# Four chunks of u normalized beside the last plain pair, two more squares on VectorE, and one low half issued later, in a hybrid attention, convolution and SwiGLU block

## The chip, the cores and the metric

The kernel runs on one core of one Trainium2 chip. The metric is the device time of one execution in microseconds (us). The kernel before was run three times. Beside those runs one execution was recorded by the hardware profiler; all durations and waits below come from that one.

## What is computed

One residual layer over 512 tokens of 2048 features, in float32. Cut to what matters here:

```python
u = rms_norm(h, mix_pre_g)
q, k, v, ca, cb, ga, gb = split(u @ w_in)
y_attn = neighbourhood_attention(q, k, v, rpb) @ w_attn_o
z = ca * sigmoid(cb)
z = depthwise_conv(z, w_dw, width=31) + b_dw
y_conv = silu(layer_norm(z, ln_g, ln_b)) @ w_conv_o
merged = sigmoid(ga) * y_attn + sigmoid(gb) * y_conv
h = h + rms_norm(merged @ w_out, mix_post_g)
u = rms_norm(h, ffn_pre_g)
gate, up = split(u @ w_gate_up)
h = h + rms_norm((silu(gate) * up) @ w_down, ffn_post_g)
```

## The kernel before

**Arithmetic.** Features lie on the 128 partitions and the 512 tokens along the free axis, so an activation is 16 tiles of 128x512. Every product of float32 values is made from halves: an operand is split into a high half (a cast to fp32r, on ScalarE, ACT) and a low half (the operand less its high half, on VectorE, DVE). A product then takes three matmuls: high by low, high by high, low by high. Weights are treated alike. `wchunk` loads 128x1024 values on SP's DMA queue into one of five buffers of the tag "raw" (L150), casts the high half on ACT (L151) and makes the low half on VectorE (L156). A raw buffer is free again when its low half has been made. `split` (L165) does the same for an activation, and `gemm` runs the three matmuls over eight k-tiles of each weight tile (L197, L200, L201).

**Taps.** The depthwise convolution has 31 taps for each of 8 tiles; each tap but the middle one is one VectorE instruction (`tap`, L470). They are not done in one go: `wchunk` ends with `taps(rate)`, which puts `rate` taps from a list behind each weight tile, in every stage from the plain pairs to the output projections. `R_CONV`, `R_V` (two halves), `R_QK` and `R_Y` set the rate by stage.

**Stages around the change.** First come the plain pairs of the gated convolution (`cb` and `ca`): tiles 0 and 1 are interleaved with the loading of x, and i = 2, 3, 4 take 16 k-tiles each for `cb` and then for `ca`. They use u without the row norm and scale the result. From v on, u is used with the norm applied: `normalize(c)` loads chunk c of x again into a raw buffer (L425, SP), multiplies it on VectorE (`un`, L526, two tiles), stores both tiles to DRAM (ACT's queue), and splits them (L165). Chunks 0 to UN_EARLY - 1 are normalized ahead of the last plain pair's weights, each other one ahead of its weights in v's first half. v has two halves of eight chunks, each of 24 matmuls (L555 to L557).

**w_out.** The product with w_out takes pairs of output tiles by a seven-product scheme of quarters (`strassen`): products named 11, 21, T2, T1, T3, 22 and T4 accumulate into banks x, y and z, with sums of weight quarters on VectorE between them (`wsum`, L280; `s4`, L341). In the first pair ("apart") the product 21 has a bank of its own. A sum p5 (L339) reads bank y after T3 and before T4 adds to it. Each product's weights get their halves in `halved_weights` (L258). The operands of the first pair come from `mr[i]`, whose last addition is on L879, followed by `operand_steps` (differences on L863, halves through `merged`, L178 and L179).

**Sum of squares.** For the FFN's norm, each of 16 tiles of the new h is squared on ACT (L977). Squares 0, 1 and KT - 4 = 12 start three accumulators; squares 2 to 11 are added to the first two by GpSimd (POOL) with accumulating DMAs (L981), and 13 to 15 to the third on VectorE (`folded`, L389). At the end VectorE adds the third and the second accumulator to the first. `rstd` sums over partitions with one-column matmuls (`r_s`, L362), VectorE scales (`r_v`, L370), GpSimd takes the power (`r_r`, L372), and `by_column` spreads the result with eight matmuls (`r_b`, L379); between `r_s` and `r_b` stand nine matmuls of the next product.

**Order.** Each engine runs its instructions in the order in which the build's scheduler puts them; where the code pins an instruction (`keep_in_program_order`) or ties it behind another (`issued_behind`), that order is fixed. Buffers of a tag go to whoever comes next in that order, when one is free.

Of the kernel before, what the change touches and what calls it, by code (L numbers as in the profile page):

```python
# [28 lines left out]
ALU = mybir.AluOpType  # L29
# [5 lines left out]
KT = D // P  # L35
# [22 lines left out]
DN_3 = DN_2 + DN_P  # L58

LN_AT = 10  # L60
R_CONV, R_V, R_QK, R_Y = 4, (3, 4), 4, 4
PLAIN = 5
TAP_K, TAP_AT = 2, ((1, 3, 5), (0, 1, 3, 5))
BEFORE = 14
# [6 lines left out]
SINGLE, SUMMED = 4, 10  # L71
COPY_AT = 10
RE_EARLY = 11
UN_EARLY, YA_EARLY = 2, 8
C_PRE, C_POST, C_FPRE, C_FPOST, C_LNG, C_LNB, C_BDW, C_WDW = 0, 16, 32, 48, 64, 72, 80, 88
C_N = C_WDW + CT * CW

# [2 lines left out]
def hybrid_block(ctx: ExitStack, tc, xT, vecs, rpb, mask, w_c0, w_qk, w_v, w_gg, w_cg, w_ao, w_co, w_out, w_g0, w_gu, w_dn, w_dl, g_post, out):  # L80
    nc = tc.nc
# [24 lines left out]
    def issued_behind(ins, other):  # L106

        tc.add_manual_dep(
            ins.ins, other.ins.name, mybir.DependencyInfo(mybir.DependencyClass.NoSync, mybir.DependencyReason.DATA),
            reason="issue order",  # L110
        )
# [139 lines left out]
        load(raw, w[:, c * 1024 : (c + 1) * 1024])  # L251
        return raw

    def halved_weights(w, name, pin=False):

        hi = wp.tile([P, 1024], F32R, tag="whi", name=f"{name}h")
        lo = wp.tile([P, 1024], F32R, tag="wlo", name=f"{name}l")
        ins = nc.scalar.copy(hi, w), nc.vector.tensor_tensor(out=lo, in0=w, in1=hi.bitcast(F32), op=ALU.subtract)  # L258
        for i in ins if pin else ():
            tc.keep_in_program_order(i)  # L260
        return hi, lo

    def begun(w0, name):
# [1 line left out]
        a11 = quarter(w0, 0, name)  # L265
        return (a11, *halved_weights(a11, name))

    def strassen(w0, w1, op, name, n, s1=None, behind_last=None, first=None, quarters=None, apart=False, turn=True, midway=None, taps_at=()):

        x, y, z = ((bank, abank)[n % 2](f"{name}_{i}") for i in range(3))

        def wsum(a, b, op, i):
            t = stp.tile([P, 1024], F32, tag="S", name=f"{name}s{i}")
            nc.vector.tensor_tensor(out=t, in0=a, in1=b, op=op)  # L280
            return t

        def copied(ps, i):
            t = stp.tile([P, NT], F32, tag="quad", name=f"{name}v{i}", bufs=3)
            nc.scalar.copy(t, ps)  # L285
            return t

        count = iter(range(7))

        def product(ps, w, b, first=False, last=False, lo_first=False):  # L290
            number = next(count)
            hi, lo = w if isinstance(w, tuple) else halved_weights(w, name)
            ws = [slice(k * P, (k + 1) * P) for k in range(HT)]
            steps = [(hi, slice(0, NT)), (lo, A)]
            if lo_first:
                steps.reverse()
            for n, (wt, cols) in enumerate(steps):
                for k, t in enumerate(op[b]):
                    mmul = nc.tensor.matmul(  # L299
                        ps[:, cols], wt[:, ws[k]], t[:, cols], start=first and n + k == 0,  # L300
                        stop=last and n + k == HT, skip_group_check=True,
                    )
                    if (n, k) == (0, TAP_K) and number in taps_at:
                        taps(1, mmul)

        def done(ps, i):
            t = stp.tile([P, HN], F32, tag="half", name=f"{name}c{i}", bufs=2)
            nc.scalar.copy(t, ps[:, B])
            return ps[:, A], t

        if quarters:
            a11, a12, a21, a22 = quarters
        elif apart:
            a11, a12, a21, a22 = (first[0], *(quarter(*w, name) for w in ((w0, 1), (w1, 0), (w1, 1))))
        s1 = s1 or sums(w1, name)
        if not apart:
            a11, a21, a12, a22 = (quarter(*w, name) for w in ((w0, 0), (w1, 0), (w0, 1), (w1, 1)))
        product(x, first[1:] if first else a11, "11", first=True)
        if apart:
            v = (bank, abank)[n % 2](f"{name}_3")  # L320
            product(v, a12, "21", first=True, last=True)
        s2 = wsum(s1, a11, ALU.subtract, 2)
        p1 = copied(x, 1)
        product(y, s2, "T2", first=True)
        product(z, s1, "T1", first=True)
        nc.vector.tensor_tensor(out=y, in0=y, in1=p1, op=ALU.add)  # L326
        u2 = copied(y, 2)
        s3 = wsum(a11, a21, ALU.subtract, 3)
        product(y, s3, "T3", lo_first=turn)
        if midway:  # L330
            midway()
        p5 = copied(z, 3)
        nc.vector.tensor_tensor(out=z, in0=z, in1=u2, op=ALU.add)
        if apart:
            nc.vector.tensor_tensor(out=v, in0=v, in1=p1, op=ALU.add)  # L335
            x = v
        else:
            product(x, a12, "21", last=True)
        nc.vector.tensor_tensor(out=p5, in0=y, in1=p5, op=ALU.add)  # L339
        s4 = s2  # L340
        nc.vector.tensor_tensor(out=s4, in0=a12, in1=s2, op=ALU.subtract)  # L341
        c11 = done(x, 1)
        product(z, s4, "22", last=True, lo_first=turn)
        c12 = None if behind_last else done(z, 2)
        product(y, a22, "T4", last=True)
        if behind_last:
            behind_last()
            c12 = done(z, 2)
        return c11, c12, done(y, 3), (p5[:, A], p5[:, B])
# [191 lines left out]
    u, v = un, []  # L541
# [125 lines left out]
    raw, uf, quarters = [], [], []  # L667
# [38 lines left out]
    first = (quarters[0], *halved_weights(quarters[0], "k0", pin=True))  # L706
# [168 lines left out]
    for i in (c + n * HT for c in range(HT) for n in range(2)):  # L875
        if i == KT - 1:
            first = begun(w_out[0], "wo0")
        mr[i] = gated(*projected(i, 1, w_co, yc))
        nc.vector.tensor_tensor(out=mr[i], in0=mr[i], in1=yg[i], op=ALU.add)  # L879

        if i < KT - 2:
            for _ in range(1 if i < HT else 5):
                next(steps[i % HT])
# [7 lines left out]
    acc = None  # L891
    for i in range(0, KT - 2, 2):
        c11, c12, c21, c22 = strassen(
            w_out[i], w_out[i + 1], op, f"wo{i}", i // 2 + 1, first=None if i else first, apart=i == 0
        )
        for n, halves_of in enumerate((((A, c11), (B, c12)), ((B, c22), (A, c21)))):
            t = slot(f"fo{i + n}")
            for cols, c in halves_of:
                joined(t[:, cols], c)
            nc.scalar.dma_start(f_d[i + n], t)  # L900
            acc = sumsq(acc, t, f"f{i + n}")
# [61 lines left out]
    for c in (*range(SPLIT), *range(HT)):  # L963
# [7 lines left out]
        for i in (2 * c, 2 * c + 1):  # L971
            h2(i, cols)
            if cols != A:
                nc.scalar.dma_start(h_d[i], f[i])

                sq = slot(f"h{i}_sq")
                nc.scalar.activation(sq, f[i], AF.Square)  # L977
                if i in (0, 1, KT - 4):
                    acc.append(sq)
                elif i < KT - 4:  # L980
                    nc.gpsimd.dma_start(acc[i % 2], sq, accum_op=ALU.add)  # L981
                else:
                    folded([acc[2], sq])
# [533 lines left out]
```

## Time and profile before

| | |
|---|---|
| median of three runs | 2481.27 us (2480.18, 2482.13, 2481.27) |
| the profiled execution's own time | 2482.7 us |
| its span in the trace | 2480.9 us |
| instructions | 35643 |
| accumulating loads' landing in the sum of squares | 5.0 to 8.8 us, median 6.7 |
| taps on z, L470 | x180, mean 765 ns |
| v weights, issue to landing | median 4.8 us |
| GpSimd's busy time | 479.5 us, 19% |

The span runs from the first to the last recorded instruction; the execution's own time has what lies around it as well. PE is TensorE's matmuls, PEld its weight loads (they overlap matmuls), DVE is VectorE, ACT is ScalarE, POOL is GpSimd, SP is SyncE, which only issues DMAs. A row of the timeline gives start, duration, engine, line, operation, output <- inputs, and in square brackets the idle time before it and what ended that. Two instructions of an engine overlap a little, so the cost of one in a full stretch is the distance between starts. Tile names are shown without their numbers where rows of several tiles are put together.

### The profile page before, as it was taken

How to read it: one execution, taken by the hardware profiler on the slowest of the kernel's cores; microseconds unless marked ns; L12 is line 12 of the kernel's file. 1: busy time of each engine (PE TensorE's matmuls, PEld its weight loads, DVE VectorE, ACT ScalarE, POOL GpSimd, SP SyncE). 2: the span in 40 equal slices, each digit the busy share in tenths (PEclk: the TensorE clock that was granted, in tenths of full speed). 3: DMA queues.
4: the chain of work that ended last, by engine and by line, in shares of the span. 5: the costliest groups of instructions: out<-in, count | busy, mean ns of one | idle time of the engine just before them, and what ended most of it. 6: DMA issues, size and time to landing. Idle time of an engine off the chain costs nothing. (4 is left out here: it accounts for less than half of the span.)

```text
span 2480.9 us, 35643 instructions
## 1 busy us (share of the span) xinstructions
PE 2458.6 (99%) x13219; PEld 2125.1 (86%) x13219; DVE 2081.9 (84%) x2754; ACT 1262.4 (51%) x1951; POOL 479.5 (19%) x576
## 2 busy tenths in 40 slices
PE   9999999999999999999999999999999999999998
PEld 8878888888888888889888888888888888888887
DVE  5998644998889778888898888889998889989886
ACT  5232333655555244556455555555555566456454
POOL 0102312200000000012111111122221203542343
PEclk9999999999999999999999999999999999999999
DMA  6363223766667544669466665666666678888987
GB/s 216 123 199 104 101 97 121 255 187 198 195 191 226 190 141 136 203 211 303 147 178 175 182 180 169 177 205 198 204 214 195 213 226 243 242 220 261 213 225 219
DMA packets 163246, 476.53 MB, mean 192 GB/s; under 512 B 18560, under 2 KB 28256, under 8 KB 163072
## 3 DMA queue, kind: packets, MB, share of 16 engines
q1 hardware_dynamic: 107200, 334.41, 40.3%
q0 software_dynamic: 34128, 101.86, 19.3%
q10 hardware_dynamic: 21744, 37.98, 4.1%
q8 instruction: 104, 1.70, 0.3%
q14 instruction: 70, 0.57, 0.1%
HBM read 400.52 MB, written 72.22 MB: 191 GB/s over the span
## 5 line engine op out<-in xcount | busy, mean ns | idle before, releaser
L470 DVE SCALAR_TENSOR_TENSOR cv<-z,vec,cv 128x497 f32<-128x497 f32 (+9 forms) x180 | 137.4, 765 | 2.8
L1054 POOL TENSOR_TENSOR row<-row,asq 128x512 f32<-128x512 f32 x30 | 55.0, 1832 | 407.6 <-ACT asq L1053 407.6
L156 DVE TENSOR_TENSOR wlo_qk<-raw_qk,whi_qk 128x1024 fp32r<-128x1024 f32 x32 | 41.2, 1287 | 61.7 <-ACT whi_qk L151 61.7
L1215 POOL TENSOR_TENSOR ys<-ys,row 128x512 f32<-128x512 f32 x32 | 57.7, 1804 | 115.8 <-DVE ys L352 107.1
L151 ACT CAST whi_qk<-raw_qk 128x1024 fp32r<-128x1024 f32 x32 | 33.6, 1051 | 81.2 <-PE qk L200 48.6
L1078 POOL TENSOR_TENSOR an<-an,row 128x512 f32<-128x512 f32 x32 | 52.2, 1631 | 75.4 <-DMA an<-a_d 49.1
L151 ACT CAST whi_y<-raw_y 128x1024 fp32r<-128x1024 f32 x31 | 32.6, 1052 | 66.4 <-PE py L200 50.9
L197 PE MATMUL py<-ycl,whi_y 128*128 128x512 f32 x128 | 49.8, 389 | 0.0
L200 PE MATMUL py<-ych,whi_y 128*128 128x512 f32 x128 | 49.8, 389 | 0.0
L201 PE MATMUL py<-ych,wlo_y 128*128 128x512 f32 x128 | 49.8, 389 | 0.0
L569 POOL TENSOR_TENSOR bm<-braw,msk 128x64 f32<-128x64 f32 x96 | 44.2, 496 | 28.7 <-DMA braw<-in_rpb 28.7
L156 DVE TENSOR_TENSOR wlo_y<-raw_y,whi_y 128x1024 fp32r<-128x1024 f32 x31 | 37.8, 1221 | 10.6 <-ACT whi_y L151 10.3
L470 DVE SCALAR_TENSOR_TENSOR cv<-zr,vec,cv 128x497 f32<-128x497 f32 (+14 forms) x60 | 45.3, 756 | 0.5
L480 POOL TENSOR_TENSOR csum<-csum,cv 128x512 f32<-128x512 f32 x7 | 12.1, 1734 | 144.4 <-DVE cv L470 144.4
L820 DVE TENSOR_TENSOR gg<-py,gg 128x512 f32<-128x512 f32 x32 | 21.7, 684 | 17.3 <-PE py L201 10.6
L631 POOL DMA_DIRECT2D att_d<-ao x8 | 4.4, 555 | 151.3 <-ACT ao L630 131.2
L606 ACT ACTIVATE sc<-sc,st 128x256 f32<-128x256 f32 x32 | 16.1, 504 | 31.4 <-DVE st L605 31.1
L1216 POOL DMA_DIRECT2D y_d<-ys x32 | 29.3, 914 | 10.4 <-POOL ys L1215 7.5
L1145 DVE TENSOR_TENSOR sg<-sg,su 128x512 f32<-128x512 f32 x39 | 30.0, 768 | 0.0
L200 PEld LDWEIGHTS py<-ych,whi_y 128*128 128x128 f32 x128 | 24.0, 188 | 5.0
L201 PEld LDWEIGHTS py<-ych,wlo_y 128*128 128x128 f32 x128 | 24.0, 188 | 5.0
L197 PEld LDWEIGHTS py<-ycl,whi_y 128*128 128x128 f32 x128 | 24.0, 188 | 4.9
(3251 smaller groups left out, 8662.9 us busy)
## 6 DMA issues: line engine op xcount, KB each, us to landing
raw_qk<-in_w_qk SPq DMA_DIRECT2D x32, 512.0 KB, 3.5
a_d<-sg ACTq DMA_DIRECT2D x41, 256.0 KB, 3.8
raw_v<-in_w_v SPq DMA_DIRECT2D x16, 512.0 KB, 4.8
gg<-g_d SPq DMA_DIRECT2D x32, 256.0 KB, 4.8
raw_y<-in_w_co SPq DMA_DIRECT2D x16, 512.0 KB, 3.6
raw_f<-in_w_g SPq DMA_DIRECT2D x16, 512.0 KB, 4.2
an<-a_d POOLq DMA_DIRECT2D x32, 256.0 KB, 5.4
as_d<-an POOLq DMA_DIRECT2D x32, 256.0 KB, 4.6
```

The lines of the kernel that those rows point to most:

```text
L151: ins = cast(hi[:, s], raw[:, s])
L156: nc.vector.tensor_tensor(out=lo[:, s], in0=raw[:, s], in1=hi[:, s].bitcast(F32), op=ALU.subtract)
L197: mmul = nc.tensor.matmul(ps, hi[:, s], al, start=first, stop=False)
L200: nc.tensor.matmul(ps, hi[:, s], ah, start=False, stop=False)
L201: nc.tensor.matmul(ps, lo[:, s], ah, start=False, stop=last)
L470: ins = nc.vector.scalar_tensor_tensor(out=a[:, to], in0=z[:, fr], scalar=col(C_WDW, i * CW + w), in1=a[:, to], op0=ALU.mult, op1=ALU.add)
L569: nc.gpsimd.tensor_tensor(out=bm[:, o + i - i0], in0=raw[:, :, min(max(i, 0), 3) * EC : (min(max(i, 0), 3) + 1) * EC], in1=msk[:, o + i - ...
L1054: nc.gpsimd.tensor_tensor(out=row[n], in0=row[n], in1=sq, op=ALU.add)
L1078: ins = nc.gpsimd.dma_start(t, a_d[DN_P + k]), nc.gpsimd.tensor_tensor(out=t, in0=t, in1=row[k // KT], op=ALU.mult)
L1145: nc.vector.tensor_tensor(out=t, in0=t, in1=up, op=ALU.mult)
L1215: tc.keep_in_program_order(nc.gpsimd.tensor_tensor(out=t, in0=t, in1=row[n], op=ALU.mult))
L1216: tc.keep_in_program_order(nc.gpsimd.dma_start(y_d[0, o], t, accum_op=ALU.add))
```

## The change

Four things are edited. `UN_EARLY` goes from 2 to 4, so chunks 2 and 3 of u are normalized ahead of the last plain pair's weights. `R_V` goes from (3, 4) to (2, 4): two taps in place of three behind each of the eight weight tiles of v's first half; the list of taps is the same, so they come later. `SUMMED_AT = 10` takes the place of KT - 4 = 12 in the sum of squares: square 10 starts the third accumulator, and 11 and 12 are added to it on VectorE. Last, the low half of a12 in w_out's first pair (the weights of product 21) is tied behind the last addition of L879.

```diff
-R_CONV, R_V, R_QK, R_Y = 4, (3, 4), 4, 4
+R_CONV, R_V, R_QK, R_Y = 4, (2, 4), 4, 4
...
-UN_EARLY, YA_EARLY = 2, 8
+UN_EARLY, YA_EARLY = 4, 8
+SUMMED_AT = 10
...
-    def halved_weights(w, name, pin=False):
+    def halved_weights(w, name, pin=False, after=None):
...
+        if after:
+            issued_behind(ins[1], after)
         return hi, lo
...
         if apart:
             v = (bank, abank)[n % 2](f"{name}_3")
-            product(v, a12, "21", first=True, last=True)
+            product(v, halved_weights(a12, name, after=after), "21", first=True, last=True)
...
-        nc.vector.tensor_tensor(out=mr[i], in0=mr[i], in1=yg[i], op=ALU.add)
+        summed = nc.vector.tensor_tensor(out=mr[i], in0=mr[i], in1=yg[i], op=ALU.add)
...
-            w_out[i], w_out[i + 1], op, f"wo{i}", i // 2 + 1, first=None if i else first, apart=i == 0
+            w_out[i], w_out[i + 1], op, f"wo{i}", i // 2 + 1, first=None if i else first, apart=i == 0,
+            after=None if i else summed,
...
-                if i in (0, 1, KT - 4):
+                if i in (0, 1, SUMMED_AT):
                     acc.append(sq)
-                elif i < KT - 4:
+                elif i < SUMMED_AT:
                     nc.gpsimd.dma_start(acc[i % 2], sq, accum_op=ALU.add)
```

The lines below L74 move down by one to four. The build reorders instructions at three places. On SP, ahead of the last plain pair (`xn` is a chunk of x, `raw_cb4`, `raw_ca4` the pair's weights, `raw_v0` those of v's first half), the kernel before has:

```order
L425 DMA xn0_809<-in_xT 128x1024
L425 DMA xn1_825<-in_xT 128x1024
L150 DMA raw_cb4_0_0_843<-in_w_cg 128x1024
L150 DMA raw_cb4_0_8_879<-in_w_cg 128x1024
L150 DMA raw_ca4_0_0_913<-in_w_cg 128x1024
L150 DMA raw_ca4_0_8_947<-in_w_cg 128x1024
L150 DMA raw_v0_0_993<-in_w_v 128x1024
L150 DMA raw_v0_1_1026<-in_w_v 128x1024
L425 DMA xn2_1059<-in_xT 128x1024
L150 DMA raw_v0_2_1075<-in_w_v 128x1024
L425 DMA xn3_1108<-in_xT 128x1024
```

And in the changed kernel the same place on SP reads:

```order
L428 DMA xn0_809<-in_xT 128x1024
L428 DMA xn1_825<-in_xT 128x1024
L428 DMA xn2_841<-in_xT 128x1024
L428 DMA xn3_857<-in_xT 128x1024
L151 DMA raw_cb4_0_0_875<-in_w_cg 128x1024
L151 DMA raw_cb4_0_8_911<-in_w_cg 128x1024
L151 DMA raw_ca4_0_0_945<-in_w_cg 128x1024
L151 DMA raw_ca4_0_8_979<-in_w_cg 128x1024
L151 DMA raw_v0_0_1025<-in_w_v 128x1024
L151 DMA raw_v0_1_1057<-in_w_v 128x1024
L151 DMA raw_v0_2_1089<-in_w_v 128x1024
```

The loads of `xn2` and `xn3` moved ahead of six weight loads. On VectorE, at w_out's first pair (`wo0_1` is bank y, `wo0_2` z, `wo0_3` the apart product's; `wo0l` are low halves of weights, `wo0s2` becomes s4, `wo0v3` p5), the kernel before has:

```order
L326 TENSOR_TENSOR wo0_1_8826<-wo0_1_8826,wo0v1_8876 128x512
L258 TENSOR_TENSOR wo0l_8924<-wo0s3_8921,wo0h_8923 128x1024
L335 TENSOR_TENSOR wo0_3_8853<-wo0_3_8853,wo0v1_8876 128x512
L258 TENSOR_TENSOR wo0l_8952<-wo0s2_8874,wo0h_8951 128x1024
L333 TENSOR_TENSOR wo0_2_8827<-wo0_2_8827,wo0v2_8919 128x512
L258 TENSOR_TENSOR wo0l_8974<-wo0q_8832,wo0h_8973 128x1024
L339 TENSOR_TENSOR wo0v3_8943<-wo0_1_8826,wo0v3_8943 128x512
```

And in the changed kernel the same stretch of VectorE is this:

```order
L259 TENSOR_TENSOR wo0l_8899<-wo0s1_8834,wo0h_8898 128x1024
L329 TENSOR_TENSOR wo0_1_8826<-wo0_1_8826,wo0v1_8876 128x512
L259 TENSOR_TENSOR wo0l_8924<-wo0s3_8921,wo0h_8923 128x1024
L338 TENSOR_TENSOR wo0_3_8853<-wo0_3_8853,wo0v1_8876 128x512
L344 TENSOR_TENSOR wo0s2_8874<-wo0q_8828,wo0s2_8874 128x1024
L336 TENSOR_TENSOR wo0_2_8827<-wo0_2_8827,wo0v2_8919 128x512
L355 TENSOR_TENSOR fo0_8995<-wo0_3_8853,wo0c1_8949 128x256
L283 TENSOR_TENSOR wo2s2_9042<-wo2s1_9011,wo2q_9014 128x1024
L342 TENSOR_TENSOR wo0v3_8943<-wo0_1_8826,wo0v3_8943 128x512
L259 TENSOR_TENSOR wo0l_8952<-wo0s2_8874,wo0h_8951 128x1024
L259 TENSOR_TENSOR wo0l_8974<-wo0q_8832,wo0h_8973 128x1024
```

The sum s4 (L344, before L341) and T1's low half (`wo0l_8899`) slid behind the operand's splits, two low halves fell behind p5 and s2 of the next pair (`wo2s2`) came ahead of it. On TensorE, a T4 operand is `mt4`, a T3 operand `mt3`; T3's last high matmuls in the kernel before are followed by product 22 (`m20_1`, `m21_1` and so on), and then by T4:

```order
L299 MATMUL wo0_1_8826<-mt3_6_8812,wo0h_8923 128x512
L299 MATMUL wo0_1_8826<-mt3_7_8815,wo0h_8923 128x512
L299 MATMUL wo0_2_8827<-m20_1_8113,wo0l_8952 128x256
L299 MATMUL wo0_2_8827<-m21_1_8211,wo0l_8952 128x256
L299 MATMUL wo0_2_8827<-m22_1_8309,wo0l_8952 128x256
```

In the changed kernel six of T4's eight high matmuls stand directly behind T3:

```order
L302 MATMUL wo0_1_8826<-mt3_6_8812,wo0h_8923 128x512
L302 MATMUL wo0_1_8826<-mt3_7_8815,wo0h_8923 128x512
L302 MATMUL wo0_1_8826<-mt4_0_8129,wo0h_8973 128x512
L302 MATMUL wo0_1_8826<-mt4_1_8227,wo0h_8973 128x512
L302 MATMUL wo0_1_8826<-mt4_2_8325,wo0h_8973 128x512
L302 MATMUL wo0_1_8826<-mt4_3_8423,wo0h_8973 128x512
L302 MATMUL wo0_1_8826<-mt4_4_8521,wo0h_8973 128x512
L302 MATMUL wo0_1_8826<-mt4_5_8619,wo0h_8973 128x512
L302 MATMUL wo0_2_8827<-m20_1_8113,wo0l_8952 128x256
L302 MATMUL wo0_2_8827<-m21_1_8211,wo0l_8952 128x256
```

What moved on TensorE is the first part of T4, from behind product 22 to ahead of it; the two remaining high matmuls and the low ones keep their place. In the stretch before `r_s` VectorE has the five adds of squares 11 to 15 in place of three, and two low halves of the next weights stand ahead of the add of square 15 where they stood behind it.

More of the change, by code (lines that the diff above doesn't have):

```diff
@@ L266, in begun, with strassen @@
         return (a11, *halved_weights(a11, name))
-    def strassen(w0, w1, op, name, n, s1=None, behind_last=None, first=None, quarters=None, apart=False, turn=True, midway=None, taps_at=()):
+    def strassen(w0, w1, op, name, n, s1=None, behind_last=None, first=None, quarters=None, apart=False, turn=True, midway=None, taps_at=(), after=None):
         x, y, z = ((bank, abank)[n % 2](f"{name}_{i}") for i in range(3))
```

## Prediction

> **What bounds the kernel now.** I read the page's busy shares first, then the list of what TensorE (PE) waited for, then windows around the places that the change touches, then the single rows there.
>
> ```profile
> PE 2458.6 (99%) x13219; PEld 2125.1 (86%) x13219; DVE 2081.9 (84%) x2754; ACT 1262.4 (51%) x1951; POOL 479.5 (19%) x576
> ```
>
> TensorE is busy for 2458.6 of the span's 2480.9 us. As long as the number of matmuls stays the same, and it does, the change can only take away waits of TensorE or add some. The list of its waits names all that are long (us in total, times, longest):
>
> ```profile
> PE r_s L362 <- DVE h_sq L389: 1.8, 1, 1.8
> ...
> PE pv L557 <- DVE un9l L165: 1.2, 1, 1.2
> PE wo L299 <- DVE m L179: 1.1, 1, 1.1
> PE pv L557 <- DVE un6l L165: 1.1, 1, 1.1
> ...
> PE r_b L379 <- POOL r_r L372: 0.3, 1, 0.3
> ```
>
> Three places carry nearly everything: `pv` (the v projection, waiting for the low halves of the normalized u), `r_s` (the FFN's sum of squares) and `wo` (w_out's first pair). All three wait for VectorE (DVE). The other waits (warm-up, the down projection, the gates) lie outside the change, and I leave them as they are.
>
> Windows of these places follow (span in us, then busy time and instructions of PE, PEld, DVE, ACT and POOL, then the granted clock of TensorE):
>
> ```profile
> 117.48:169.38 51.90, 47.50 (x197) 35.92 (x196) 51.44 (x70) 16.93 (x24) 4.04 (x3) 1.00 0.69 219
> 169.38:212.00 42.62, 42.62 (x190) 35.28 (x188) 36.71 (x47) 10.77 (x13) 2.14 (x2) 1.00 0.33 114
> 976.00:990.00 14.00, 12.89 (x75) 10.97 (x74) 13.97 (x28) 9.84 (x19) 0.91 (x1) 1.00 0.29 93
> 1187.70:1191.10 3.40, 3.40 (x9) 2.62 (x8) 1.17 (x2) 0.00 (x0) 1.95 (x1) 0.50 0.87 245
> 1191.10:1194.50 3.40, 3.40 (x20) 2.96 (x19) 1.67 (x4) 1.22 (x3) 0.00 (x0) 1.00 0.31 125
> ```
>
> In v's first half (the first row) VectorE is busy 51.44 of 51.90 us: it is the bound there. In the second half TensorE is busy throughout, 42.62 us for 188 weight loads, or 0.2267 us a matmul. At that pace v's 384 matmuls take 87.05 us, and the two rows span 94.52: 7.47 us are lost, nearly all in the first half. At w_out's first pair VectorE is full too (13.97 of 14.00). Behind the sum of squares the clock stood at 0.50 for 3.40 us, so that stretch costs 1.70 us beside the wait.
>
> **The change in v.** One chunk of the first half on VectorE, and where TensorE meets it:
>
> ```profile
> 126.87 0.74 DVE L526 SCALAR_TENSOR_TENSOR un<-xn,vec,r 128x512 f32<-128x512 f32 x1
> 127.53 1.22 DVE L156 TENSOR_TENSOR wlo_v<-raw_v,whi_v 128x1024 fp32r<-128x1024 f32 x1
> 128.66 0.74 DVE L470 SCALAR_TENSOR_TENSOR cv<-z,vec,cv 128x506 f32<-128x506 f32 x1
> 129.32 0.68 DVE L165 TENSOR_TENSOR un4l<-un,un4h 128x512 fp32r<-128x512 f32 x1
> 130.06 0.50 PE L557 MATMUL pv<-whi_v,un4l 128*128 128x512 f32 x1 [0.65 <-DVE un4l L165]
> ```
>
> From start to start `un` takes 0.66 us, the weights' low part 1.13, a tap 0.66; the split's 0.68 less the same overlap is 0.60. A chunk that still normalizes has two `un`, two splits, one low part and three taps: 1.32 + 1.20 + 1.13 + 1.98 = 5.63 us of VectorE, against 24 x 0.2267 = 5.44 of TensorE. With two taps it is 4.97, and for the two chunks that now come normalized it is less. So from chunk 4 on VectorE gains 0.47 us a chunk on TensorE where it lost 0.19, and the waits for `un6l` and `un9l` should go. The eight taps (5.3 us) slide into v's second half, where VectorE has 5.9 us free of 42.62, and from there into the query/key stage; I count nothing for them, since no wait there is in the list, and if that cover were gone they would cost at most their 5.3.
>
> What is moved earlier is not free. The two x loads of chunks 2 and 3 now stand on SP's queue ahead of all weights of the last plain pair, and they hold two more of five raw buffers until VectorE's `un` reads them, which in VectorE's order stays where the first `un` was, about 103 us. Four x tiles leave one buffer for the pair's four weight loads. Each load must then wait until the low part of the load before has been read: load, cast, low part, and again. The rows for this:
>
> ```profile
> 84.10 1.22 DVE L156 TENSOR_TENSOR wlo_ca<-raw_ca,whi_ca 128x1024 fp32r<-128x1024 f32 x1
> 85.35 6.50 SPq L150 DMA_DIRECT2D raw_ca<-in_w_cg  x2
> L151 ACT CAST whi_ca<-raw_ca x6: 1045/1054/1057, 50.5 to 104.8; 128x1024 fp32r<-128x1024 f32 x6
> 106.60 0.39 PE L197 MATMUL ca<-u0l,whi_ca 128*128 128x512 f32 x1
> DMA to landing us min/median/max: 3.0/4.2/6.5
> ```
>
> The last row is that of `raw_ca`. A cycle is a landing L plus 1.05 (cast) plus 1.22 (low part) plus some 0.13 of hand-over, L + 2.40. The buffer comes free at 85.35; the fourth low part is ready at 85.35 + 4 (L + 2.40). It is needed when `ca`'s ninth k-tile starts its third matmul: 106.60 + 8 x 0.68 + 0.46 = 112.50. The stall is thus 4L - 17.55 if nothing else delays it: none up to L = 4.39, 8.45 at the maximum of 6.5. With the median of 4.2 the fourth low part would be just in time. VectorE's rows between (taps of 0.66, `un` and splits, since the low part is not at their head) make two of the cycles longer; followed through in its order, the fourth load is issued near 105.8. There it meets x and u traffic, where a weight tile of v took this long:
>
> ```profile
> raw_v<-in_w_v SPq DMA_DIRECT2D x1, 512.0 KB, 4.9
> ```
>
> So it lands near 110.7, is cast by 111.85 and split by 113.2: TensorE loses some 0.9 us (bounds 0 and 2.5, for landings of 4.2 to 6.5 of this one load). The four u stores move with their chunks, on ACT's queue, where it has room (16.93 of 51.90 busy): nothing. A further 0.5 us I allow for one late `un` near the first half's end, where margins are 0.4 to 1.7 us. Sum for v: 7.47 - 0.9 - 0.5 = **6.1 us gained** (bounds 3.5 and 7.5).
>
> **The sum of squares.** The rows that end it now, in order of time by engine:
>
> ```profile
> 1174.58 0.86 POOL L981 DMA_DIRECT2D h_sq<-h_sq  x1 [3.28 <-DMA h_sq<-h_sq]
> 1178.05 0.86 POOL L981 DMA_DIRECT2D h_sq<-h_sq  x1 [2.61 <-DMA h_sq<-h_sq]
> 1187.82 1.95 POOL L372 TENSOR_TENSOR r_r<-r_v,mhalf 128x4 f32<-128x4 f32 x1 [8.90 <-DVE r_v L370]
> 1179.03 0.69 DVE L389 TENSOR_TENSOR h_sq<-h_sq 128x512 f32<-128x512 f32 x1 [0.64 <-ACT h_sq L977]
> 1181.73 0.69 DVE L389 TENSOR_TENSOR h_sq<-h_sq 128x512 f32<-128x512 f32 x1 [2.01 <-DMA h_sq<-h_sq]
> 1185.67 0.69 DVE L389 TENSOR_TENSOR h_sq<-h_sq 128x512 f32<-128x512 f32 x1 [2.11 <-DMA h_sq<-h_sq]
> 1184.28 0.39 PE L214 MATMUL f<-u_15l,whi_f 128*128 128x512 f32 x1
> 1186.51 1.02 PE L362 MATMUL r_s<-ones,h_sq 128*128 128x1 f32 x8 [1.84 <-DVE h_sq L389]
> 1191.11 1.06 PE L379 MATMUL r_b<-ident,r_r 128*128 128x128 f32 x8
> ```
>
> GpSimd's last two accumulating transfers (tiles 10 and 11) land at 1181.7 and 1185.6, and VectorE's two last adds wait for them. With tiles 10 and 11 on VectorE the last transfers are those of 8 and 9, which had landed when the next were issued: 1174.58 and 1178.05. What is late next is VectorE itself. The add of tile 15 ended at 1179.72; ahead of it now stand two more adds (1.2 us) and two low parts of weights (2 x 1.13) that before stood behind, less the 0.64 it waited: 1182.5, and the two last adds (1.2) end near 1183.7. TensorE could start `r_s` at 1184.5, so a margin of some 0.7 us is left and the wait goes: 2.0 us. The reciprocal root then shows: in before GpSimd's `r_r` ended at 1189.77, 3.26 behind `r_s`' start. After, `r_s` takes 0.88, nine matmuls at full clock 2.04, and `r_b`, possible 3.35 behind `r_s`' start at 1187.85, waits some 0.4. Against 1191.11 that is **3.2 us gained**, if the half clock goes with the wait. Bounds: 1.0 (clock stays, VectorE a microsecond late) and 3.7 (`r_b` unwaited).
>
> The clock is the open part: among these windows 0.50 stands only here, right behind 2.0 us of idle and 0.9 of one-column matmuls, and 1.00 behind the waits of 1.1 to 1.2. I take it that it goes. The Trainium skill, "TensorE: Matmul & The Clock Gate", section "Part 1: The HAM clock gate (the "warmup" mystery)", says that the clock halves after at least one idle window of about 3.4 us. By that rule 2.0 us alone would not do it, the cause would lie elsewhere and the stretch could stay; the gain here would be some 2.0.
>
> **w_out's first pair.** The rows of TensorE, then VectorE:
>
> ```profile
> 981.33 0.50 PE L299 MATMUL wo<-m,wo0h 128*128 128x512 f32 x1 [1.11 <-DVE m L179]
> 991.18 1.11 PE L299 MATMUL wo<-m,wo0l 128*128 128x256 f32 x8
> 996.74 2.00 PE L299 MATMUL wo<-m,wo2h 128*128 128x512 f32 x8
> 977.99 1.21 DVE L258 TENSOR_TENSOR wo0l<-wo0s,wo0h 128x1024 fp32r<-128x1024 f32 x1
> 986.96 1.21 DVE L258 TENSOR_TENSOR wo0l<-wo0s,wo0h 128x1024 fp32r<-128x1024 f32 x1
> 988.09 0.69 DVE L335 TENSOR_TENSOR wo<-wo,wo0v 128x512 f32<-128x512 f32 x1
> 991.56 0.68 DVE L339 TENSOR_TENSOR wo0v<-wo,wo0v 128x512 f32<-128x512 f32 x1
> ```
>
> The low part of a12 behind `summed` lets the last operand's add and split run about 1.1 us sooner, so the wait at 981.33 shrinks to near nothing: a gain of 1.1. But VectorE is full, and the same work comes due a few microseconds later: `T3`'s low part (row 986.96) ends no sooner, near 988.0, as two low parts slid behind and a cast is waited for. So `T3` starts 0.1 earlier at best, and the 1.1 is waited away. Then comes the new order: `T4`'s first matmuls stand directly behind `T3` on TensorE, and they write the accumulator that the add of L339 must read first. That add can't start before `T3` ends, near 991.0, and on VectorE it stands behind an add, `s4`, an add, a half add and the next pair's `s2`: 988.0 + 0.6 + 1.13 + 0.6 + 0.35 + 1.13 = 991.8, done 992.5. In before, the `22` product filled exactly this time. TensorE waits some 1.6 us, `wo2` starts near 998.3 where it was 996.74: **1.5 us lost** (bounds: 1.1 gained if nothing of this bites, 2.5 lost if a cast comes late too).
>
> **Sum.** 6.1 + 3.2 - 1.5 = 7.8 us. The profiled execution took 2482.7 us (span 2480.9), 1.4 above the median of the runs, 2481.27; it would become 2474.9, and the median 2473.5.
>
> **The rivals.** (a) *w_out gains.* If VectorE reaches the add of L339 as soon as `T3` ends, or `T4`'s wait hides, the 1.1 stays: 6.1 + 3.2 + 1.1 = 10.4, 2470.9. For it: 1.11 is a real wait. Against: 13.97 of 14.00 us busy. Chance 0.13.
> (b) *The sum of squares yields less.* Half clock stays, or the fold ends a microsecond late: 2.0 or 1.0 in place of 3.2, total 6.6 to 5.6, 2474.7 to 2475.7. For it: only 0.7 us of margin, and a clock whose cause one place can't settle; 2.0 is the wait alone. Chance 0.15. The rule of the Trainium skill quoted above would end here.
> (c) *Slower: weights late through one buffer.* If landings run long with two x tiles more ahead of them, the stall of 4L - 17.55 grows, and waits over 2 us bring half clock at 1.7 us each. With two such stretches the change breaks even where 4L - 17.55 + 3.4 + 0.5 = 7.47 + 3.2 - 1.5, at L = 5.7; at L = 7.0 it loses 10.45 + 3.4 + 0.5 - 9.17 = 5.2, 2486.5. For it: the 6.5 maximum; against: the median 4.2, and 4.9 beside traffic. Chance 0.05.
> (d) *The change does not do what it says.* VectorE is still last in v's first half, since the two early chunks' 5 us only move ahead of a full stretch, and v gains 3.5; with 1.0 to 3.2 at the squares and the loss of 1.5 the total is 3.0 to 5.2, 2478.3 to 2476.1. For it: VectorE was full there; against: eight taps really leave. Chance 0.12.
>
> **How the numbers follow.** The forecast itself has 0.55, and its time is 2473.5. Adding the gains' upper bounds that are likely together (7.5, 3.2 and 1.1) gives 11.8, 2469.5; the lower end takes (d) in half its width, 2478.0. A measurement of this kernel can tell about 0.2%, 5.0 us, from no change: faster means below 2476.3. Nearly all of the forecast (0.53) and of (a) (0.13), most of (b) (0.13) and little of (d) (0.02) lie there, 0.81; slower by as much is left to half of (c), 0.03; the rest is 0.16.
>
> **What would show it.** Right: no `pv` waits for `un` left, v's two windows at 88 to 89 us; a small new wait of `ca` for the cast or low part near 112; `r_s` without a wait, clock 1.00 behind it and `r_b` waiting 0.3 to 0.5 for `r_r`; at w_out the wait on `m` gone and a new one of `wo` on L339's add (a few lines lower now) of about 1.6. Wrong: a wait of `cb` or `ca` of several microseconds with half clock behind it; `h_sq` still last at `r_s`; no wait behind `T3`, with `wo2`'s first matmul some 1.1 earlier than before, counted from the pair's start.

## The result, and the profile after

The changed kernel is faster. Sixteen runs of each gave a median of 2477.51 us (2475.65 to 2478.90) against 2483.21 (2479.64 to 2486.43); the ratio is 0.9976, with a 95% interval of 0.9968 to 0.9984, or 4.0 to 7.9 us. The forecast, 7.8 us less, lies at the far end of that interval; the measured middle is 5.7. The forecast time, 2473.5, was counted from before's first three runs, whose median lay 1.9 us below that of the sixteen, so the differences are what can be compared. The profiled execution of the changed kernel has a span of 2476.7 us, 4.2 below that of before (its own time, 2478.54, is a microsecond above its median, where before's was half a microsecond below that of its sixteen runs).

Where the 4.2 us of the two profiles come from is read by laying the starts of the same matmuls beside each other:

| stretch | before, us | after, us | difference | forecast |
|---|---|---|---|---|
| start to v's first matmul | 117.48 | 118.58 | +1.10 | +0.9 |
| v, first matmul to the first of query/key | 94.52 | 88.52 | -6.00 | -7.0 |
| query/key and attention, heads 0 and 1 (mainly) | | | +1.95 | 0 |
| gates, convolution, projections | | | -0.39 | 0 |
| w_out, first matmul to the second pair's first | 21.06 | 23.66 | +2.60 | +1.5 |
| rest of w_out to `r_b` (the sum of squares) | | | -3.60 | -3.2 |
| all behind it | | | +0.14 | 0 |

The waits of TensorE in the changed kernel, as they answer to the list of before (in total, times, longest):

```profile
PE po L629 <- DVE ptl L627: 1.5, 2, 0.8
PE wo L302 <- DVE wo0v L342: 1.4, 1, 1.4
PE d L302 <- ACT d_0v L288: 1.3, 1, 1.3
PE pv L560 <- DVE un15l L166: 1.2, 1, 1.2
PE wo L302 <- DVE m L180: 0.9, 1, 0.9
PE wo L302 <- ACT wo0v L288: 0.6, 1, 0.6
...
PE ca L202 <- DVE wlo_ca L157: 0.5, 1, 0.5
```

The five waits in v for low halves are one; `r_s` no longer waits for `h_sq`; the new ones for `wlo_ca` and for p5 (`wo0v`, L342) were forecast. Not in the forecast's sum: `po` waits for attention (1.5), the wait on `m`, said to shrink to near nothing, is still 0.9, and one of w_out's products waits 0.6 for a cast, which stood in the forecast's lower bound alone. The wait of `d`, in the down projection, lies outside the change (1.1 before). The single rows of TensorE in v and the heads, and with them the window of v (columns as in the prediction):

```profile
113.46 0.50 PE L202 MATMUL ca<-u8h,wlo_ca 128*128 128x512 f32 x1 [0.53 <-DVE wlo_ca L157]
161.17 0.50 PE L560 MATMUL pv<-whi_v,un15l 128*128 128x512 f32 x1 [1.17 <-DVE un15l L166]
241.16 0.39 PE L629 MATMUL po<-ptl,v_0h 128*128 128x256 f32 x1 [0.80 <-DVE ptl L627]
293.04 0.38 PE L629 MATMUL po<-ptl,v_0h 128*128 128x256 f32 x1 [0.66 <-DVE ptl L627]
118.58:207.10 88.52, 87.35 (x385) 71.99 (x384) 81.71 (x107) 28.56 (x37) 6.94 (x5) 1.00 0.57 187
```

Shortly ahead of each of the last three of these matmuls, an instruction of VectorE takes a microsecond too long. Three stretched rows of the changed kernel follow, each with what GpSimd (POOL) runs beside it; a tap takes 0.73 elsewhere, two scalings 0.61, one 0.34:

```profile
158.74 1.77 DVE L473 SCALAR_TENSOR_TENSOR cv<-z,vec,cv 128x497 f32<-128x497 f32 x1
157.84 2.14 POOL L483 TENSOR_TENSOR csum<-csum,cv 128x512 f32<-128x512 f32 x1 [23.48 <-DVE cv L473]
237.65 1.67 DVE L611 TENSOR_SCALAR sc<-sc,st 128x256 f32<-128x256 f32 x2
237.88 1.29 POOL L483 TENSOR_TENSOR csum<-csum,cv 128x512 f32<-128x512 f32 x1 [19.40 <-DVE cv L473]
290.04 1.42 DVE L611 TENSOR_SCALAR sc<-sc,st 128x256 f32<-128x256 f32 x1
290.01 1.29 POOL L483 TENSOR_TENSOR csum<-csum,cv 128x512 f32<-128x512 f32 x1 [9.82 <-DVE st L610]
```

GpSimd adds a convolution tile to `csum` when its last tap is done. The three additions here are those of tiles 1, 3 and 4 (that of tile 0 is a copy). In the kernel before, those of tiles 3 and 4 fell beside a low half of weights, where a microsecond was to spare; that of tile 3:

```profile
229.38 1.87 DVE L156 TENSOR_TENSOR wlo_qk<-raw_qk,whi_qk 128x1024 fp32r<-128x1024 f32 x1 [0.65 <-ACT whi_qk L151]
228.87 1.29 POOL L480 TENSOR_TENSOR csum<-csum,cv 128x512 f32<-128x512 f32 x1 [5.85 <-DVE cv L470]
```

The addition of tile 1 fell in v's first half before as well. It lengthened a tap there too, ahead of the longest of v's waits in the kernel before (VectorE, GpSimd, TensorE):

```profile
145.92 1.66 DVE L470 SCALAR_TENSOR_TENSOR cv<-z,vec,cv 128x498 f32<-128x498 f32 x1
145.38 1.66 POOL L480 TENSOR_TENSOR csum<-csum,cv 128x512 f32<-128x512 f32 x1 [25.69 <-DVE cv L470]
148.23 0.50 PE L557 MATMUL pv<-whi_v,un9l 128*128 128x512 f32 x1 [1.23 <-DVE un9l L165]
```

So this microsecond only moved within v, from `un9l` to `un15l`. Moving eight taps later moved the ends of tiles 3 and 4 to places in the heads where VectorE is waited for. At w_out, the rows of TensorE and the row with which VectorE's work begins there:

```profile
972.34 1.98 PE L302 MATMUL wo<-m,wo0h 128*128 128x512 f32 x8
977.81 0.50 PE L302 MATMUL wo<-m,wo0h 128*128 128x512 f32 x1 [0.93 <-DVE m L180]
985.93 1.19 PE L302 MATMUL wo<-mt,wo0l 128*128 128x256 f32 x8 [0.62 <-ACT wo0v L288]
990.33 1.63 PE L302 MATMUL wo<-mt,wo0h 128*128 128x512 f32 x6 [1.37 <-DVE wo0v L342]
996.00 2.00 PE L302 MATMUL wo<-m,wo2h 128*128 128x512 f32 x8
969.00 0.69 DVE L823 TENSOR_TENSOR gg<-py,gg 128x512 f32<-128x512 f32 x1 [4.42 <-DMA gg<-g_d]
```

And the same beginning in the kernel before, TensorE's first matmul of w_out and VectorE's row:

```profile
975.68 1.98 PE L299 MATMUL wo<-m,wo0h 128*128 128x512 f32 x8
971.25 0.69 DVE L820 TENSOR_TENSOR gg<-py,gg 128x512 f32<-128x512 f32 x1 [3.32 <-DMA gg<-g_d]
```

VectorE starts there when a gate tile `gg` has landed: 4.43 us ahead of w_out's first matmul in the kernel before, 3.34 ahead in the changed one. This distance is called the lead below; it shrank because TensorE comes 3.3 us earlier, the gate tile only 2.25. Last, the sum of squares in the changed kernel (VectorE's last adds, TensorE, GpSimd's root, the low half beside it, TensorE again, and the window from `r_s` to `r_b`):

```profile
1181.05 2.13 DVE L392 TENSOR_TENSOR h_sq<-h_sq 128x512 f32<-128x512 f32 x3
1183.78 0.95 PE L365 MATMUL r_s<-ones,h_sq 128*128 128x1 f32 x8
1185.01 1.03 POOL L375 TENSOR_TENSOR r_r<-r_v,mhalf 128x4 f32<-128x4 f32 x1 [15.24 <-DVE r_v L373]
1185.12 1.23 DVE L157 TENSOR_TENSOR wlo_f<-raw_f,whi_f 128x1024 fp32r<-128x1024 f32 x1 [0.19 <-ACT whi_f L152]
1186.77 1.05 PE L382 MATMUL r_b<-ident,r_r 128*128 128x128 f32 x8
1183.78:1186.77 2.99, 2.99 (x18) 2.58 (x17) 1.39 (x2) 1.05 (x1) 1.03 (x1) 1.00 0.57 198
```

The adds end at 1183.18, 0.6 us ahead of `r_s`; `r_s` doesn't wait, the clock is 1.00, and the root took 1.03 us where it had taken 1.95, so `r_b` doesn't wait either. Before, a low half of VectorE had begun 0.18 us ahead of the root (at 1187.64); here the low half begins 0.11 us behind it.

### The profile page after: what moved, and what is told of

The parts are those of the page before. It is cut to its first block, busy times and chain, and to the rows that moved or that the text cites. A ratio compares the mean times of both kernels' runs of the same rounds, so it can differ in the third digit from the quotient of the medians.

```text
span 2476.7 us, 35648 instructions
## 1 busy us (share of the span) xinstructions
PE 2454.9 (99%) x13219; PEld 2123.7 (86%) x13219; DVE 2080.8 (84%) x2756; ACT 1262.5 (51%) x1951; POOL 481.9 (19%) x574
```

## The experiments

All are edits of the changed kernel; each was timed against the kernel before on the same chip. "Stretch" is from w_out's first matmul to the second pair's first, "v" from its first matmul to the first of query/key. Single edits are judged by these stretches: the intervals of the ratios are some 0.001 wide to each side, and spans of two profiles differ by one or two microseconds where no edit reaches. The wait of `d` on `d_0v` in the down projection was between less than 0.2 and 1.6 us long in these runs, and the first `r_s` of the kernel started between 50.2 and 51.9 us.

**The tie alone undone.**

```diff
-            after=None if i else summed,
```

> The changed kernel without the tie of a12's low half, the other three edits kept. Theory: the tie brings six of T4's matmuls directly behind T3, where they wait for p5, and costs 2.6 us; without it the stretch from w_out's first matmul to the second pair's first falls from 23.66 us to before's 21.1, with one wait on m of about 1.1 left, and the profiled span from 2476.7 to about 2474.1. Rival: the tie gains its 1.1 and the loss in that stretch comes from elsewhere (the phase at which the stretch is entered); then the stretch stays at 23.7 or gets longer, and the span is 2476.7 or more.

Measured: 2476.59 us, ratio 0.9977 [0.9968, 0.9985], span 2475.7. The stretch is 23.73, so neither theory held in full; the microsecond by which the span is shorter lies in the down projection, whose wait of 1.3 us is missing in this run. T4 stands behind product 22 again and doesn't wait, but the wait on `m` is far longer than before's 1.11, and the clock is at 0.54 behind it (rows and windows of this run; the last three numbers of a window are the clock, the share of the DMA engines that was busy, and GB/s):

```profile
979.44 0.80 PE L302 MATMUL wo<-m,wo0h 128*128 128x512 f32 x1 [2.53 <-DVE m L180]
976.90:979.40 2.50, 0.00 (x1) 0.00 (x0) 2.50 (x5) 1.45 (x4) 0.00 (x0) 0.94 0.00 0
979.44:982.80 3.36, 3.36 (x13) 3.05 (x13) 3.36 (x9) 2.54 (x8) 0.00 (x0) 0.54 0.42 156
969.36 0.69 DVE L823 TENSOR_TENSOR gg<-py,gg 128x512 f32<-128x512 f32 x1 [4.80 <-DMA gg<-g_d]
```

The gate tile landed 2.96 us ahead of w_out's first matmul (972.32) here. Lead and wait add up to 5.49 without the tie (5.54 in the kernel before) and to 4.27 with it. So the tie does bring `m` forward, by 1.25 us, and the landing decides how much of a wait is left.

**Three taps again, four chunks early.**

```diff
-R_CONV, R_V, R_QK, R_Y = 4, (2, 4), 4, 4
+R_CONV, R_V, R_QK, R_Y = 4, (3, 4), 4, 4
```

> The changed kernel with three taps again behind each weight tile of v's first half, four chunks still early. Theory A (the eight taps carry v's gain, since VectorE was full before v too and the early chunks' work only moves within a full stretch): from the first matmul of v to the first of query/key 93 to 95 us, as before's 94.5 and not 88.5, waits on the low halves of un back, the wait of ca for its weights still there; span near 2482. Theory B (the early chunks carry it): 88.5 to 90 us, span 2476 to 2478.

Measured: 2481.84 us, ratio 0.9997 [0.9988, 1.0006], span 2480.7; v takes 94.35 us, with this among its waits:

```profile
151.74 0.50 PE L560 MATMUL pv<-whi_v,un10l 128*128 128x512 f32 x1 [1.98 <-DVE un10l L166]
151.74:155.10 3.36, 3.30 (x13) 2.47 (x14) 3.36 (x5) 1.57 (x2) 0.00 (x0) 1.00 0.70 196
```

Theory A: with three taps the early chunks gain nothing in v (94.52 before). The window behind this wait of 1.98 us has the full clock.

**Two chunks early, two taps.**

```diff
-UN_EARLY, YA_EARLY = 4, 8
+UN_EARLY, YA_EARLY = 2, 8
```

> The changed kernel with two chunks early as before, two taps in v's first half kept. Theory A (the taps carry the gain, the early chunks only cost a buffer): v takes 88 to 90 us, and the waits of ca for its last weight tile (0.7 us, 1.3 with what follows) go, so the span is 2475 to 2477. Theory B (the early chunks carry it): v takes 92 to 94 us and the span is 2480 to 2482.

Measured: 2479.36 us, ratio 0.9988 [0.9979, 0.9997], span 2477.7. The wait of `ca` is gone (v starts at 117.70), and v takes 91.01, between the theories. Its largest wait:

```profile
159.32 0.50 PE L560 MATMUL pv<-whi_v,un14l 128*128 128x512 f32 x1 [1.72 <-DVE un14l L166]
```

The taps carry 3.5 of v's 6.0 us by themselves; the early chunks add 2.5 once there is room, and cost 1.3 at `ca` (counted from the first `r_s` to v's first matmul). Behind the wait of 1.72 us the clock is 1.00.

**csum by accumulating DMAs.**

```diff
-                nc.gpsimd.tensor_tensor(out=csum, in0=csum, in1=a, op=ALU.add)
+                nc.gpsimd.dma_start(csum, a, accum_op=ALU.add)
```

> The changed kernel with GpSimd's addition of each finished convolution tile to csum done by an accumulating DMA, so that GpSimd runs no arithmetic there. Theory: an instruction of VectorE that runs beside such an addition takes 1.04 us longer (a tap 1.77 for 0.73 at 158.7, two scalings 1.67 for 0.61 at 237.7, one 1.42 for 0.34 at 290.0), and this is what ends late in front of un15l and of po in heads 0 and 1; then these stretched instructions go, the waits of 1.17, 0.80 and 0.66 fall below 0.2 each, and the span drops by 2.3 to 3.0 to about 2474. Rival: VectorE is late there from the eight taps that slid back, whatever GpSimd does; the waits stay and the span is 2476 to 2477.

Measured: 2482.11 us, ratio 0.9998 [0.9989, 1.0006], span 2480.3. All three waits are gone and v takes 87.44 us; up to `po` of head 1 TensorE is 3.9 us ahead of the changed kernel (0.9 of it because the late weights of `ca` landed in 4.5 us for 5.5). Then the last tile's transfer stands in the way, and 7 us are lost there, with the clock at 0.51 for 3.4 us behind the wait:

```profile
845.69 2.07 PE L777 MATMUL pmu<-csum,ones 128*128 128x512 f32 x2 [5.07 <-DMA csum<-cv]
```

So the cause of the three waits is shown: it is the additions on GpSimd. This kernel as a whole gains nothing; the mixed csum, below, mends that.

**The gates' loads ahead of the second pair's weights.**

```diff
+    def load_behind_gates(out, src):
+
+        issued_behind(nc.sync.dma_start(out, src), g_loads[-1])
...
-            a11, a21, a12, a22 = (quarter(*w, name) for w in ((w0, 0), (w1, 0), (w0, 1), (w1, 1)))
+            a11, a21, a12, a22 = (quarter(*w, name, load) for w in ((w0, 0), (w1, 0), (w0, 1), (w1, 1)))
...
-            after=None if i else summed,
+            after=None if i else summed, load=load_behind_gates if i == 2 else nc.sync.dma_start,
```

> The changed kernel with the three weight loads of w_out's second pair put behind the last loads of the gates on SP's queue (the same transfers, another order). Theory: the wait on m at w_out's first pair is not set by the order of VectorE's low halves but by the gate tile gg, whose load stands behind 1 MB of weights of the second pair and lands 3.0 to 4.4 us ahead of w_out's first matmul, differently in every run; with the load ahead, VectorE starts there a microsecond or more sooner and the wait of 0.93 goes, the wait of T4 on p5 (1.37) stays: stretch from w_out's first matmul to the second pair's 22.0 to 22.8 us for 23.66. Rival: the wait on m stays at 0.6 to 1.3, since VectorE is full there whatever lands; stretch 23.5.

Measured: 2476.19 us, ratio 0.9974 [0.9963, 0.9985], span 2475.3. VectorE no longer waits for a gate tile, the wait on `m` is gone, and the stretch is 21.32 us, shorter than expected, since T3's wait of 0.62 went too. The ratio can't be told from the changed kernel's 0.9976. What is left in the stretch:

```profile
988.63 1.62 PE L302 MATMUL wo<-mt,wo0h 128*128 128x512 f32 x6 [1.38 <-DVE wo0v L342]
```

**The same, and the tie undone.**

```diff
-            after=None if i else summed,
+            load=load_behind_gates if i == 2 else nc.sync.dma_start,
```

> As the run with the gates' loads first, and without the tie of a12's low half, so that T4 stands behind product 22 again on TensorE. Theory (the tie costs the T4 wait, the landing the rest): no wait on m over 0.5, no wait on p5, stretch 20.0 to 21.0 us, where before had 21.06 and the changed kernel 23.66. Rival (the tie itself shortens the wait on m): the wait on m is 1 us or more here and shorter in the tied run.

Measured: 2475.28 us, ratio 0.9972 [0.9961, 0.9982], span 2475.1. No wait on `m` and none on p5, as the theory had it. But the build put the second pair's first matmul ahead of product 22, where it waits for its cast:

```profile
988.27 0.50 PE L302 MATMUL wo<-m,wo2h 128*128 128x512 f32 x1 [1.18 <-ACT wo2h L259]
```

So the stretch (to the second pair's other matmuls) is 21.2 us, and the run doesn't tell what T4's wait alone is worth.

**The old split of the squares.**

```diff
-SUMMED_AT = 10
+SUMMED_AT = 12
```

> The changed kernel with squares 10, 11 on GpSimd's accumulating DMAs as before. Theory: the wait at r_s of 1.8 and the half clock behind it come back together, from the start of r_s' possible slot to r_b 6.5 us for 3.0, span 2480.0 to 2480.6. Rival (the half clock had another cause, at another time): the wait comes back and the clock behind it is 1.00, so that only 2.0 us are lost, span 2478.7.

Measured: 2480.24 us (2478.10 to 2484.80), ratio 0.9993 [0.9984, 1.0002], with a span of 2476.3 in the profile, which is of the fastest of its eleven runs. The wait came back at half its length: `r_s` waits 0.87, and the clock stays at 1.00, as the rival had it:

```profile
1183.75 1.02 PE L365 MATMUL r_s<-ones,h_sq 128*128 128x1 f32 x8 [0.87 <-DVE h_sq L392]
```

Its last add still waits for a transfer, so the wait varies with the landing. By the ratios the edit is worth some 4 us, give or take 3 (0.9993 against 0.9976, each within 0.0009), in this profile 1.35. What the squares cost in the slower of these runs was not profiled.

**A late sum without transfers.** The total of the squares is multiplied by one on GpSimd and passed through a maximum with itself on VectorE; its value stays.

```diff
+    total = folded([acc[0], acc[2], acc[1]])
+    s = total[0].rearrange("p (n t) -> p n t", n=NB)
+    nc.gpsimd.tensor_tensor(out=s, in0=s, in1=ones[:, None, :].broadcast_to([P, NB, P]), op=ALU.mult)
+    nc.vector.tensor_tensor(out=total[0], in0=total[0], in1=total[0], op=ALU.max)
-    r3, r = slot("r3"), rstd(folded([acc[0], acc[2], acc[1]]), D, "r3", pin=True)
+    r3, r = slot("r3"), rstd(total, D, "r3", pin=True)
```

> The changed kernel with two operations more on the total of the squares that leave it as it is (GpSimd times one, VectorE the maximum with itself), so that r_s is late by some 1.5 to 2.2 us with no transfer involved. Theory (idle time of about 2 us and one-column matmuls halve the clock): 0.50 for about 3.4 us behind r_s, as in before. Rival (the clock's rule needs some 3.4 us of idle time, or the transfers' traffic had a part): the wait alone, clock 1.00 behind it.

Measured: 2480.78 us, ratio 0.9992 [0.9983, 1.0000], span 2478.4. The wait came out at 1.48 and left the clock at 1.00 (row, and the window from `r_s` to `r_b`):

```profile
1186.09 1.02 PE L365 MATMUL r_s<-ones,h_sq 128*128 128x1 f32 x8 [1.48 <-DVE h_sq L992]
1186.09:1189.41 3.32, 3.22 (x17) 2.48 (x18) 1.30 (x2) 0.00 (x0) 1.96 (x1) 1.00 0.08 27
```

**A later sum without transfers.** The same with the maximum taken twice. This kernel was run once.

> The changed kernel with three operations more on the total of the squares (GpSimd times one, VectorE twice the maximum with itself), so that r_s waits about 2.1 us with no transfer involved, where a wait of 1.48 left the clock at 1.00. Theory (a length between 1.5 and 1.8 decides): clock 0.50 behind it for some 3.4 us. Rival (the transfers' traffic or the phase decides): 1.00.

Measured: 2482.53 us, span 2480.8. The wait is 2.20, and the clock is at half through `r_s`, the nine matmuls and `r_b`, 7.0 us in all:

```profile
1185.84 1.71 PE L365 MATMUL r_s<-ones,h_sq 128*128 128x1 f32 x8 [2.20 <-DVE h_sq L993]
1185.84:1191.39 5.55, 5.55 (x18) 4.68 (x18) 1.15 (x2) 0.00 (x0) 1.03 (x1) 0.51 0.34 123
1191.39:1192.88 1.49, 1.49 (x9) 1.49 (x8) 0.00 (x0) 0.00 (x0) 0.00 (x0) 0.52 0.00 0
```

No transfer ends this wait, and the half clock follows all the same.

**csum mixed.** Tiles 1 to 6 by accumulating DMA, the last by GpSimd's addition.

```diff
-                nc.gpsimd.tensor_tensor(out=csum, in0=csum, in1=a, op=ALU.add)
+                if i == CT - 1:
+                    nc.gpsimd.tensor_tensor(out=csum, in0=csum, in1=a, op=ALU.add)
+                else:
+                    nc.gpsimd.dma_start(csum, a, accum_op=ALU.add)
```

> The changed kernel with tiles 1 to 6 of the convolution added to csum by accumulating DMAs and the last tile by GpSimd's addition as before. Theory (the stretched instructions of VectorE set the three late waits; only the last transfer's landing, 5 us, lost it again): no waits on un15l and on po over 0.2, none on csum, span 2.6 to 3.9 below the changed kernel's 2476.7, that is 2472.8 to 2474.1. Rival (something later gives it back whatever ends there): span 2476 or more.

Measured: 2474.59 us, ratio 0.9969 [0.9956, 0.9981], span 2473.0. The three waits and that of the last tile are gone; v takes 87.46. Of the 3.7 us by which the span is below the changed kernel's, 1.3 lie in the down projection, whose wait is missing here. The two scalings that had taken 1.67 us, and GpSimd's row in the same place:

```profile
236.49 0.61 DVE L614 TENSOR_SCALAR sc<-sc,st 128x256 f32<-128x256 f32 x2
236.87 0.89 POOL L486 DMA_DIRECT2D csum<-cv  x1 [19.55 <-DVE sc L614]
```

**All four together.** The mixed csum, the gates' loads first, no tie, and the second pair's first matmul held behind T4:

```diff
+                    if name == "wo2" and number == n == k == 0:
+                        issued_behind(mmul, products[-1])
...
+            products.append(mmul)
```

> The changed kernel with the mixed csum, the gates' loads ahead of the second pair's weights, no tie of a12's low half, and the second pair's first matmul kept behind T4. Theory (the places add up): 2.8 from csum, and a stretch from w_out's first matmul to the second pair's of 19.9 to 20.4 us for 23.66; span 2470.0 to 2471.0. Rival (TensorE arrives earlier at the next load and waits there): stretch 21 us or more, span 2472 to 2474.

Measured: 2472.27 us, ratio 0.9958 [0.9946, 0.9971], span 2469.3, a little below what was expected. The stretch is 20.64, a little more than expected, with one wait in it:

```profile
983.60 1.21 PE L304 MATMUL wo<-m,wo0l 128*128 128x256 f32 x8 [0.87 <-DVE wo0l L259]
```

**All four, three chunks early.**

```diff
-UN_EARLY, YA_EARLY = 4, 8
+UN_EARLY, YA_EARLY = 3, 8
```

> As the run before, with three chunks of u early. Theory A (the fourth early chunk only takes the raw buffer on which ca waits): the wait of ca of 0 to 1.3 us goes, v takes 87.5 us still, span 0.3 to 1.3 lower. Theory B (VectorE needs all four): v takes 88.5 to 90 us, span higher by up to 2.

Measured: 2470.08 us, ratio 0.9951 [0.9937, 0.9965]: the fastest version, 12 us below the kernel before. v takes 87.36 us, and no wait of `ca` is left: theory A for the wait and for v. The profiled execution (span 2472.0) was the slowest of its five; of the 2.7 us that it has over the run before, 1.3 lie ahead of the first `r_s` and some 1.0 in a wait of the gates' products. The intervals of these last two runs overlap, so that the third chunk's saving over the fourth is shown by the stage, not by the total.

## Why the prediction was right, and where it was off

**v: right, with the reasons mis-weighed.** The gain was 4.9 us (6.0 less the later start of 1.1) for 6.1. The wait of `ca` on its last weight tile came where and as worked out: the fourth load was issued at 105.5 (105.8 was given), landed in 5.5 us where 4.9 was taken, and cost 1.28 with what follows. In the ten runs with four chunks early and two taps, that load landed in 4.46 to 5.51 us, and the losses, from 0.26 to 1.28, rise with it (from the first `r_s` to v's first matmul, against before's 67.15): each is about the landing less 4.2, where the bounds had put nothing lost at 4.2. What failed is the allowance of 0.5 for a late `un` near the half's end: v lost 1.47 against its full pace, and 1.04 of that was a tap that ran beside GpSimd's addition, as one had in the kernel before. The 5.63 us of VectorE counted for a chunk leave that out. Of the 6.0 us the taps gave 3.5 alone, and the early chunks nothing without them.

**The eight taps: the step "I count nothing for them" failed.** They cost 1.95 us in heads 0 and 1, and it isn't their own duration: with GpSimd's additions made transfers, the taps stay where they are and the waits go. What they moved was the moment at which a convolution tile ends. In the profile of before, the tap of 1.66 us at 145.92 and the low half of 1.87 at 229.38 would have told that an addition can cost VectorE such time.

**The squares: right.** No wait, full clock, 3.6 us for 3.2; the 0.4 is `r_b`, which didn't wait because the root on GpSimd took 1.03 us for 1.95. What the old split costs varies, though: its wait was 1.84 in the profile of before and 0.87 in another run. That the half clock goes with TensorE's idle time, and not with the transfers, is shown now: it came behind a wait that no transfer ended (2.20) and behind one in which the DMA engines' share was 0.00 (2.53). How long the idle time must be is not: waits of 0.87 to 1.48 left 1.00 behind them, and so did 1.72 and 1.98 in v, while waits of 1.84, 2.20, 2.53 and 5.07 brought about half. So the length alone doesn't decide between 1.8 and 2.0 us. What else does, such as the moment at which the wait falls or the matmuls around it, stays open. The rule of the Trainium skill ("TensorE: Matmul & The Clock Gate", section "Part 1: The HAM clock gate (the "warmup" mystery)") that an idle window of some 3.4 us is needed does not fit the waits of 1.84 to 2.53; the measurement decides. That the half clock then lasts about 3.4 us, or about twice that behind the wait of 2.20 (7.0), does agree with the window that the page gives.

**w_out: the sign right, the size 2.6 for 1.5.** The wait of T4 on p5 was 1.37 where 1.6 was worked out. What failed is "the wait at 981.33 shrinks to near nothing": it was 0.93, because VectorE starts this work on a gate tile's landing, and TensorE's gain of 3.3 us ahead of it had eaten 1.1 of the lead. In the eight runs with the tie and the gates' old loads, lead and stretch add up to 27.0 us each time, from 2.99 and 23.99 to 4.41 and 22.59. With before's lead of 4.43 the stretch would thus be 22.57, 1.5 longer than before's 21.06: the size that was forecast. The 1.1 that the forecast missed is the lead that was lost. The tie is worth the 1.25 us it was written for and costs the T4 order; taking it out alone left the stretch as long as it was (23.73), with half clock in it, and the times as they were within the intervals.

**The rivals.** Slower by late weights: the mechanism is real, but it held for one load of the four, and the longest landing seen there was 5.5 us. The rival in which v's gain was halved did not come, but its reason holds for the early chunks alone, which gained 0.2 us with three taps; that of the squares did not come either. Between the two profiles the total of 7.8 missed by the heads (1.95), v (1.2) and the lead at w_out (1.1); the squares, 0.4 better, and the other stages, 0.25 better, took some of that back. The upper end of the range, 2478.0, is given as (d) in half its width; the middle of (d)'s 2476.1 to 2478.3 would be 2477.2.

## What to carry to other kernels

When a change lets the bounding engine arrive earlier, look up what the next stages wait for that does not move with it: here a gate tile's landing gave back a third of the gain. When work is moved along a list, the events tied to its ends move too; here an addition on GpSimd cost VectorE 0.65 to 1.1 us wherever it fell, and some places had that to spare. A scheduler's answer to a tie is read from the order it prints, before the wait that the tie removes is counted as gained.

## What the runs showed of the hardware

- An instruction of VectorE that starts beside GpSimd's addition of two 128x512 tiles takes longer, in these rows by 0.65 to 1.08 us: 1.77 for 0.73 (tap), 1.67 for 0.61, 1.42 for 0.34, and 1.87 for 1.22 (low half). With the addition issued as an accumulating DMA by the same engine, the two scalings took 0.61. Where VectorE's instruction has begun first, it is GpSimd's that takes longer: the root took 1.95 us for 1.03. The Trainium skill, "SBUF — State Buffer", section "Who interferes with whom", says that an instruction of VectorE with two SBUF inputs, or in a mode that uses both ports, and one of GpSimd that reads SBUF exclude each other; the rows of taps and low halves, which have two tiles as inputs, agree with it. Whether the scalings ran in such a mode the traces do not show.
- An accumulating DMA into one tile has a price at its end: 5.07 us of TensorE's wait when the last of the chain is needed at once, none when the last is an addition.
- Landings of the same load at the same place differ from run to run by a microsecond (the weights of `ca`, 4.5 to 5.5 us in ten runs), and the waits behind them with it; a single profile is no price. The three shortest of the ten are those of the kernels with accumulating DMAs for `csum`, all of which come later in the kernel; whether that is chance is not shown.
